# Weight sums of the first up tile by adding DMAs, its norm factor in the second tile, and a final factor kept in PSUM

## The chip, the core and the metric

The kernel runs on one core of one Trainium2 chip. The metric is the device time of one execution in microseconds (us); lower is better. Five engines work side by side, each with its own queue: TensorE (PE, matmuls into PSUM), VectorE (DVE), ScalarE (ACT), GpSimd (POOL) and SyncE (SP, which only issues DMAs). ACT and POOL issue DMAs too.

## The reference

One layer of a decoder trunk, in float32, on 512 tokens of width 2048: a mixer of three head groups, a cross-attention into 256 memory tokens, a gated MLP with a causal convolution of width 3, and a final norm. What the change touches is the MLP and the final norm:

```python
def rms_norm(x, g):
    return x * rsqrt(mean(x * x, axis=-1) + EPS) * g

def conv_ffn(h, w_up, conv_w, conv_b, w_down):      # D_FF = 5504 = 43 tiles of 128
    val, gate = split(h @ w_up, 2, axis=-1)
    gp = pad(gate, two zero tokens in front)
    g = conv_b + sum(conv_w[i] * gp[:, i:i + S] for i in range(3))
    return (silu(g) * val) @ w_down

x = x + hybrid_mixer(rms_norm(x, norm_mix), ...)
x = x + memory_cross_attention(rms_norm(x, norm_cross), mem_n, ...)
x = x + conv_ffn(rms_norm(x, norm_ffn), w_up, conv_w, conv_b, w_down)
return rms_norm(x, norm_final)
```

## The kernel before

Everything is kept transposed: a tile has 128 features on the partitions and the tokens along the free dimension. The residual x lies in 16 tiles of 128x512 (`self.x1`, called str in the profile).

**Precision.** Each operand of a matmul is split in two parts, hi (ScalarE copies it, rounded) and lo (VectorE subtracts: L316/L317 and L341/L342 for weights, tiles whi and wlo with 5 buffers each). A product is three matmuls (hi x hi, lo x hi, hi x lo; L355 to L357). So each 128x512 piece of weights costs one ScalarE and one VectorE operation. Weights come through five buffers `wraw` of 128x1024, loaded on SP's queue.

**The up projection** (`up`, 43 tiles f) computes val and gate of two halves of the tokens by a scheme of seven products in place of eight. The products are numbered 1 to 7. Their left sides are the four units of the tile's weights (b11, b12, b22, b21, units 4f to 4f + 3 of `w_up`, 512 KB each) and sums of them: product 5 takes b11 + b12, product 6 b11 + b12 + b22, product 4 b11 + b12 + b22 + b21, product 7 b12 + b22. In each tile VectorE makes these four sums in place, as 128x1024 additions (L1180, L1185 and helper line L1256). Their right sides are sums of token blocks of x (`token_sums`, tiles called sum), made once while the cross-attention's output projection (`w_co`) runs. The products collect in PSUM tiles acc (products 1, 6, 7), psE or acc (2), psC (5 and 3) and psD (4).

**The first up tile** is begun in `cross`: its products 1, 2, 5 and 6 stand there between the last token sums, in the order `UP_ORDER` = 1, 5, 2, 6, 3, 4, 7 of the sums. `one(0)` in `up` takes the rest over through `self.first`. The norm factor R of the MLP's input isn't put into the weights' right sides; it is multiplied into the gate at L1300 and into the down projection's output. It comes from the squares of x, which ScalarE makes (xsqt, three buffers) and which POOL's adding DMAs collect in two tiles sq (L1140). `rms` adds over the partitions (four matmuls into psT, L450/L451, which `behind()` queues behind the last product on PE), loads ScalarE's table for Ln and Exp, and `root` makes R by Ln, Exp (L463, L464) and three VectorE operations (L465 to L467). In tile 0 `rms` is called between products 3 and 4.

Behind its products each tile has the work on the gate: gate times R (L1300), three convolution steps (L1302 to L1304), Silu, times val, and a store to DRAM (gd).

**The end.** The last three blocks of the down projection are done for each half of the tokens on its own (`finish(hf, dt)`, psD, 16 tiles dt of 128x256): VectorE adds the product to x (L1399), ScalarE squares it, VectorE and POOL collect the squares (fsq). `write(hf)` then makes x times gain times R into tiles o of two dt each and sends them out, 256 KB a DMA, on SP's and ACT's queues by turns; POOL multiplies some dt (L1418), for which ScalarE has put the gain into x (L1407), VectorE the others (L1420). The first half's writing runs between the second half's `finish` calls. For the second half the squares are added by L1437 on PE, then `root`, then `write(1)` ends the kernel.

**Order.** A planner orders each engine's instructions before the run, by readiness in its own model of time and then by place in the program; `issue_after` pins an instruction behind another one on its engine. Engines then run their queues in order.

Of the kernel before, what the change touches and what calls it, by code (L numbers as in the profile page):

```python
# [40 lines left out]
FT = D_FF // P  # L41
# [18 lines left out]
WR = 5  # L60
# [13 lines left out]
H0 = 4  # L74
H1 = 6
ST = 4
FINE = 2
E0 = 14
E1 = 1
W0 = 6  # L80
# [133 lines left out]
class _Trunk:  # L214
# [222 lines left out]

        return rs, spread

    def rms(self, parts, n, pool, after=None):  # L440

        nc = self.nc
        ss = self.pst("T")[:, :n]
        for i, a in enumerate(parts):
            hi = self.wp.tile([P, n], F32R, name="shi", tag="whi", bufs=WS, padded_shape=[P, 512])
            lo = self.wp.tile([P, n], F32R, name="slo", tag="wlo", bufs=WS, padded_shape=[P, 512])
            last = nc.scalar.activation(hi, a, AF.Copy)
            nc.vector.tensor_tensor(lo, a, hi.bitcast(F32), op=ALU.subtract)
            with self.behind():
                nc.tensor.matmul(ss, self.onesr, hi, start=(i == 0), stop=False)  # L450
                nc.tensor.matmul(ss, self.onesr, lo, start=False, stop=(i == len(parts) - 1))  # L451
        self.log_table(after or last)
        return self.root(ss, n, pool, *parts)
# [5 lines left out]
    def root(self, ss, n, pool, r, u):  # L459

        nc = self.nc
        R = pool.tile([P, n], F32, name="R", tag="R", bufs=1)
        nc.scalar.activation(r, ss, AF.Ln, scale=1.0 / D, bias=self.eps)  # L463
        nc.scalar.activation(r, r, AF.Exp, scale=-0.5)  # L464
        nc.vector.scalar_tensor_tensor(u, ss, D * EPS, r, op0=ALU.add, op1=ALU.mult)  # L465
        nc.vector.scalar_tensor_tensor(u, u, -0.5 / D, r, op0=ALU.mult, op1=ALU.mult)
        nc.vector.scalar_tensor_tensor(R, u, 1.5, r, op0=ALU.add, op1=ALU.mult)  # L467
        return R

# [520 lines left out]
    def cross(self):  # L990
# [29 lines left out]
        for i, u in enumerate(first):  # L1020
            more((i >= H0) + (i >= H1))
            u()
            if i == ST:
                R = self.rms(self.sqs, S, self.con)
        more(KT)
        self.es_mp.close()
        es_o, es_w = ExitStack(), ExitStack()
# [60 lines left out]
        def evac_q(h, t0, tn):  # L1088
# [54 lines left out]
        for u in range(8):  # L1143
            w = ws[u]
            pss = [self.acc(), self.acc()]
            for half in range(2):
                for k in range(4):
                    wh, wl = w((half * 4 + k) * P, P)
                    self.mm3(pss[half], wh, wl, oT[k][0], oT[k][1], k == 0, k == 3)
                dt = 2 * u + half  # L1150
                x1 = self.x1[dt]
                nc.vector.tensor_tensor(x1, pss[half], x1, op=ALU.add)
            if u + 2 < 8:
                ws.append(self.weights(d["w_co"][u + 2]))
            elif u == 6:
                b11, b12 = [self.up_raw(i) for i in (0, 1)]
                w1 = self.halves(b11)
            else:
                b21, b22 = [self.up_raw(i) for i in (3, 2)]
                es_o.close()  # L1160
                self.es_fa = ExitStack()
                put(self.pool(self.es_fa, "fa", "left"), own)
            if u % 2:
                part = self.token_sums(u // 2, wx, place)
                if u < 7:
                    for j in UP_ORDER:
                        part(j)
            if u:
                squares(2 * u - 2)
# [4 lines left out]
        part(1)  # L1174
        self.product(1, w1, pa, True, True)
        nc.scalar.activation(s1, pa, AF.Copy)
        w2 = self.halves(b21)
        part(2)
        self.product(2, w2, pe, True, True)
        nc.vector.tensor_tensor(b11, b11, b12, op=ALU.add)  # L1180
# [4 lines left out]
        nc.vector.tensor_tensor(b11, b11, b22, op=ALU.add)  # L1185
# [37 lines left out]
    def up_raw(self, u, pool=None):  # L1223
        if pool:
            t = pool.tile([P, 1024], F32, name="b22", tag="b22", bufs=2)
        else:
            t = self.wp.tile([P, 1024], F32, name="wraw", tag="wraw", bufs=WR)
        self.nc.sync.dma_start(out=t, in_=self.d["w_up"][u])
        return t

    def halves(self, w):
# [10 lines left out]
    def up(self):  # L1242

        nc, d = self.nc, self.d
# [3 lines left out]
        for g in gps:  # L1248
            nc.gpsimd.memset(g[:, 0:2], 0.0)
        lo, hi = slice(0, HT), slice(HT, S)  # L1250

        def cw(i, f):
            return self.conv[:, i * FT + f:i * FT + f + 1]

        def tt(out, a, b, op):
            nc.vector.tensor_tensor(out, a, b, op=op)  # L1256
# [4 lines left out]
        def one(f):  # L1261
            u2, val, gp = tmp("u2"), tmp("val", S, 2), gps[f % 2]
            pd = self.pst("D")[:, :HT]
            if f == 0:
                b11, b12, b21, b22, pb, pc, pe, s1, s5 = self.first
# [18 lines left out]
            tt(b12, b12, b22, ALU.add)  # L1284
# [5 lines left out]
            if f == FT - 1:  # L1290
                self.early = [self.wp.tile([P, 2, S], F32, name="wraw", tag="wraw", bufs=WR) for _ in range(2)]
                for i, t in enumerate(self.early):
                    for k in range(2):
                        nc.sync.dma_start(out=t[:, k, :], in_=self.gd[2 * i + k])
            self.product(7, self.halves(b12), pb, False, True)
            u3 = tmp("u2")
            tt(u3, s1, pb, ALU.subtract)
            tt(val[:, hi], u3, pd, ALU.add)
            tt(gp[:, 2 + HT:], u3, s5, ALU.add)
            nc.vector.scalar_tensor_tensor(gp[:, 2:], gp[:, 2:], -1.0, self.R, op0=ALU.mult, op1=ALU.mult)  # L1300
            c = fb.tile([P, S], F32, name="cv", tag="cv", bufs=2)
            nc.scalar.activation(c, gp[:, 0:S], AF.Identity, scale=cw(0, f), bias=cw(3, f))  # L1302
# [20 lines left out]
    def ffn(self):  # L1323
# [67 lines left out]
        def finish(hf, dt):  # L1391
# [11 lines left out]
                sqs[1].append(sq)  # L1403
            else:
                self.square(dt, x, sqs[hf], lambda n: fp.tile([P, n], F32, name="fsqt", tag="fsqt", bufs=2))
            if dt % 4 == 3 or (hf == 0 and dt % 2):
                nc.scalar.activation(x, x, AF.Copy, scale=self.gain(3, dt))  # L1407
            return added

        def write(hf):  # L1410
            tok = toks[hf]
            R = spreads[hf]
            for dt in range(0, KT, 2):
                o = fp.tile([P, 2, tw], F32, name="o", tag="o", bufs=7)
                for i in range(2):
                    x = self.x1[dt + i][:, tok]
                    if (dt + i) % 4 == 3 or (hf == 0 and i):
                        nc.gpsimd.tensor_tensor(o[:, i, :], x, R, op=ALU.mult)  # L1418
                    else:
                        nc.vector.scalar_tensor_tensor(o[:, i, :], x, self.gain(3, dt + i), R,  # L1420
                                                       op0=ALU.mult, op1=ALU.mult)
                    if hf and dt < FINE:
                        (nc.sync if i else nc.scalar).dma_start(out=self.out[(dt + i) * P:(dt + i + 1) * P, tok],
                                                                in_=o[:, i, :])
                if hf == 0 or dt >= FINE:
                    dst = self.out[dt * P:(dt + 2) * P, tok].rearrange("(i p) t -> p i t", p=P)
                    (nc.sync if dt % 4 else nc.scalar).dma_start(out=dst, in_=o)
                yield

        spreads = {}  # L1430
        w0 = write(0)
# [49 lines left out]
```

## Time and profile before

| | us |
|---|---|
| runs: median (lowest to highest) of 3 | 2361.35 (2359.89 to 2363.28) |
| the profiled execution | 2363.64 |
| its span, first to last instruction | 2361.7 |
| PE busy | 2333.6 |
| DVE busy | 1646.7 |
| ACT busy | 1135.6 |
| POOL busy | 95.4 |

The mean granted TensorE clock is 0.995 of full speed. All times of rows are counted from the span's start. A busy share is a mean over stages; what the change can do is read from the stages that it touches: the first up tile (1009 to 1039 us) and the end (from 2310 us). In a row of a timeline stand the start, the duration, the engine, the line, the operation with output and inputs, the shape, and in brackets how long the engine was idle before and what released it.

### The profile page before, as it was taken

The numbers are of one execution on the slowest core, as the hardware profiler recorded it, in microseconds if no ns is written. First come the engines' busy times: TensorE is split into PE (matmuls) and PEld (weight loads), VectorE is DVE, ScalarE is ACT, GpSimd is POOL, SyncE is SP. The second block draws the span as 40 slices with busy tenths as digits, with TensorE's granted clock in tenths as the row PEclk, the third lists the DMA queues.
The fourth block names the chain that finished last, engine by engine and source line by source line (L and its number), as shares of the span: only waits on it lengthen the run. The fifth ranks groups of instructions, "written<-read, shape, count | busy, mean of one in ns | idle before, by whom it ended". The sixth has DMA issues, their size and how long they took to land.

```text
span 2361.7 us, 38190 instructions
## 1 busy us (share of the span) xinstructions
PE 2333.6 (99%) x14514; PEld 2110.2 (89%) x14514; DVE 1646.7 (70%) x3062; ACT 1135.6 (48%) x2201; POOL 95.4 (4%) x112
## 2 busy tenths in 40 slices
PE   9999999999999999999999999999999999999997
PEld 8798898888878888889999999999999988888887
DVE  7725666667796365898888888888899844343336
ACT  6323345556664254765555555555555532232224
POOL 2000000000002000100000000000000000000003
PEclk9999999999999999999999999999999999999999
DMA  6432122322224343443333333333333443242332
GB/s 208 144 94 88 48 96 90 98 85 94 90 78 155 125 144 117 106 131 121 121 121 121 121 121 121 121 121 120 117 119 118 162 138 125 98 156 95 111 107 72
DMA packets 88452, 272.84 MB, mean 116 GB/s; under 512 B 10012, under 2 KB 14764, under 8 KB 88268
## 3 DMA queue, kind: packets, MB, share of 16 engines
q1 hardware_dynamic: 77200, 250.45, 32.1%
q10 hardware_dynamic: 7772, 12.09, 1.6%
q0 software_dynamic: 3296, 7.87, 1.4%
q8 instruction: 114, 1.87, 0.3%
q14 instruction: 70, 0.57, 0.1%
HBM read 251.18 MB, written 19.45 MB: 115 GB/s over the span
## 4 chain that ended last, share of the span: by engine, by line
PE 94%; DVE 3%; ACT 1%; POOL 1%; DMA 1%; issue 1%; DVEq 0%; SPq 0%; POOLq 0%; ACTq 0%
PE acc L355 18%; PE acc L356 18%; PE acc L357 18%; PE psC L355 3%; PE psC L357 3%; PE psC L356 3%; PE acc L398 3%; PE acc L396 3%; PE acc L397 3%; PE psD L357 2%; PE psD L355 2%; PE psD L356 2%; PE psV L355 2%; PE psU L356 2%; PE psV L356 2%; PE psU L355 2%
## 5 line engine op out<-in xcount | busy, mean ns | idle before, releaser
L342 DVE TENSOR_TENSOR wlo<-wraw,whi 128x512 fp32r<-128x512 f32 (+2 forms) x496 | 333.6, 677 | 413.8 <-ACT whi L341 406.0
L341 ACT ACTIVATE whi<-wraw 128x512 fp32r<-128x512 f32 (+2 forms) x496 | 304.1, 617 | 624.2 <-PE acc L356 366.9
L316 ACT ACTIVATE whi<-wraw 128x512 fp32r<-128x512 f32 x518 | 308.3, 627 | 307.0 <-DVE wraw L1256 161.7
L355 PE MATMUL acc<-xhi,whi 128*128 128x512 f32 (+1 forms) x1088 | 428.9, 395 | 0.0
L357 PE MATMUL acc<-xhi,wlo 128*128 128x512 f32 (+1 forms) x1088 | 423.8, 390 | 0.0
L356 PE MATMUL acc<-xlo,whi 128*128 128x512 f32 (+1 forms) x1088 | 423.2, 389 | 0.0
L317 DVE TENSOR_TENSOR wlo<-wraw,whi 128x512 fp32r<-128x512 f32 x518 | 348.1, 687 | 74.9 <-ACT whi L316 65.8
L357 PE MATMUL acc<-sum,wlo 128*128 128x256 f32 x1368 | 384.9, 281 | 0.1
L356 PE MATMUL acc<-sum,whi 128*128 128x256 f32 x1368 | 384.7, 281 | 0.0
L355 PE MATMUL acc<-sum,whi 128*128 128x256 f32 x1368 | 384.3, 281 | 0.0
L357 PEld LDWEIGHTS acc<-sum,wlo 128*128 128x128 f32 x1368 | 258.0, 189 | 0.6 <-DVE wlo L317 0.6
L356 PEld LDWEIGHTS acc<-sum,whi 128*128 128x128 f32 x1368 | 257.9, 189 | 0.2
L355 PEld LDWEIGHTS acc<-sum,whi 128*128 128x128 f32 x1368 | 257.8, 188 | 0.0
L357 PEld LDWEIGHTS acc<-xhi,wlo 128*128 128x128 f32 x1088 | 205.3, 189 | 42.7 <-issue 0.8
L356 PEld LDWEIGHTS acc<-xlo,whi 128*128 128x128 f32 x1088 | 205.5, 189 | 39.9 <-issue 1.6
L355 PEld LDWEIGHTS acc<-xhi,whi 128*128 128x128 f32 x1088 | 205.4, 189 | 38.8 <-issue 0.8
L357 PE MATMUL psC<-sum,wlo 128*128 128x256 f32 x688 | 193.7, 282 | 0.5 <-DVE wlo L317 0.5
L356 PE MATMUL psC<-sum,whi 128*128 128x256 f32 x688 | 193.0, 280 | 0.4 <-DVE sum L1217 0.4
L355 PE MATMUL psC<-sum,whi 128*128 128x256 f32 x688 | 193.4, 281 | 0.0
L356 PEld LDWEIGHTS psC<-sum,whi 128*128 128x128 f32 x688 | 129.9, 189 | 0.6 <-DVE sum L1217 0.6
L357 PEld LDWEIGHTS psC<-sum,wlo 128*128 128x128 f32 x688 | 129.5, 188 | 0.7 <-DVE wlo L317 0.7
L355 PEld LDWEIGHTS psC<-sum,whi 128*128 128x128 f32 x688 | 129.9, 189 | 0.0
(347 smaller groups left out, 4287.4 us busy)
## 6 DMA issues: line engine op xcount, KB each, us to landing
wraw<-in_w_up SPq DMA_DIRECT2D x130, 512.0 KB, 4.5
wraw<-in_w_dn SPq DMA_DIRECT2D x80, 512.0 KB, 3.7
b<-in_w_up SPq DMA_DIRECT2D x42, 512.0 KB, 3.9
wraw<-in_w_o SPq DMA_DIRECT2D x32, 512.0 KB, 3.6
wraw<-in_w_qka SPq DMA_DIRECT2D x24, 512.0 KB, 3.7
gd<-cv SPq DMA_DIRECT2D x43, 256.0 KB, 2.1
wraw<-in_w_qkb SPq DMA_DIRECT2D x16, 512.0 KB, 3.7
xraw<-in_xT SPq DMA_DIRECT2D x15, 512.0 KB, 3.9
```

The lines of the kernel that those rows point to most:

```text
L316: nc.scalar.activation(hi, r, AF.Copy)
L317: nc.vector.tensor_tensor(lo, r, hi.bitcast(F32), op=ALU.subtract)
L341: nc.scalar.activation(hi, r, AF.Copy)
L342: nc.vector.tensor_tensor(lo, r, hi.bitcast(F32), op=ALU.subtract)
L355: nc.tensor.matmul(out, lh, rh, start=start, stop=False, skip_group_check=more)
L356: nc.tensor.matmul(out, lh, rl, start=False, stop=False, skip_group_check=more)
L357: last = nc.tensor.matmul(out, ll, rh, start=False, stop=stop, skip_group_check=more)
L396: self.nc.tensor.matmul(o, xh[:, tt], wh, start=(k == 0), stop=False)
L397: self.nc.tensor.matmul(o, xh[:, tt], wl, start=False, stop=False)
L398: self.last = self.nc.tensor.matmul(o, xl[:, tt], wh, start=False, stop=(k == KT - 1))
```

## The change

- `first_sums` makes the sums of the first up tile in DRAM: for products 5, 6, 4 and 7 a plain DMA copies the first unit into a DRAM tile (pre5, pre6, pre4, pre7), and seven adding DMAs add the others, all on POOL's queue. It is called in `cross` before the queries' projection (w_cq).
- The first tile then loads seven units on SP's queue, where it loaded four, and VectorE makes no sum of weights there.
- `rms` is cut in three (`sums_of`, `log_table`, `root`). In tile 0 `sums_of` stands behind product 4; `root`, and the gate's work of tile 0 (`gate`), stand in tile 1 between its products 1 and 5.
- At the end R goes to PSUM (`self.acc()`), ScalarE copies it to SBUF for POOL (Rs), the results are written over x, and each dt goes out by a DMA of its own, 128 KB. POOL takes the dt with dt % 3 == 2 in the first half (5 in place of 8) and dt % 5 == 4 in the second (3 in place of 4).

```diff
-    def rms(self, parts, n, pool, after=None):
+    def rms(self, parts, n, R, after=None):
+        ss = self.sums_of(parts, n)
+        self.log_table(after or self.high)
+        self.root(ss, n, R, *parts)
+        return R
...
+        first = self.first_sums()
         for h in range(X_HEADS - 1):
             self.run(self.out_units(d["w_cq"], h, hs, evac_q(h, 0, NT)), W_X)
...
             elif u == 6:
-                b11, b12 = [self.up_raw(i) for i in (0, 1)]
-                w1 = self.halves(b11)
+                w1 = self.halves(self.up_raw(first[1]))
             else:
-                b21, b22 = [self.up_raw(i) for i in (3, 2)]
+                raws = [self.up_raw(first[j]) for j in (2, 5, 6)]
...
-        nc.vector.tensor_tensor(b11, b11, b12, op=ALU.add)
-        w5 = self.halves(b11)
+        w5 = self.halves(raws[1])
...
-        nc.vector.tensor_tensor(b11, b11, b22, op=ALU.add)
-        w6 = self.halves(b11)
+        w6 = self.halves(raws[2])
...
-        self.first = b11, b12, b21, b22, pb, pc, pe, s1, s5
+        self.first = [self.up_raw(first[j]) for j in (3, 4, 7)], pb, pc, pe, s1, s5
+
+    def first_sums(self):
+
+        nc, w = self.nc, self.d["w_up"]
+        terms = {5: (0, 1), 6: (0, 1, 2), 4: (0, 1, 2, 3), 7: (1, 2)}
+        src = {1: w[0], 2: w[3], 3: w[2]}
+        for j in terms:
+            src[j] = self.dr.tile([P, 1024], F32, name="pre%d" % j)
+            nc.gpsimd.dma_start(out=src[j], in_=w[terms[j][0]])
+        for i in (1, 2, 3):
+            for j in terms:
+                if i < len(terms[j]):
+                    nc.gpsimd.dma_start(out=src[j], in_=w[terms[j][i]], accum_op=ALU.add, max_dma_last_dim=1024)
+        return src
...
                 tt(b11, b11, b12, ALU.add)
+                if f == 1:
+                    self.root(self.ss, S, self.R, *self.sqs)
+                    gate(*self.late)
                 self.product(5, self.halves(b11), pc, True, True)
...
             if f == 0:
-                self.R = self.rms(self.sqs, S, self.con)
-            tt(b11, b11, b21, ALU.add)
-            self.product(4, self.halves(b11), pd, True, True)
...
+                w4 = self.halves(t4)
+                self.product(4, w4, pd, True, True)
+                self.ss = self.sums_of(self.sqs, S)
+                w7 = self.halves(t7)
+                self.log_table(self.high)
+                self.product(7, w7, pb, False, True)
...
-            if dt % 4 == 3 or (hf == 0 and dt % 2):
+            if on_pool(hf, dt):
                 nc.scalar.activation(x, x, AF.Copy, scale=self.gain(3, dt))
             return added
+        def on_pool(hf, dt):
+            return dt % 5 == 4 if hf else dt % 3 == 2
+
         def write(hf):
             tok = toks[hf]
...
+            R, Rs = spreads[hf], fp.tile([P, tw], F32, name="R", tag="R", bufs=1)
+            nc.scalar.activation(Rs, R, AF.Copy)
+            for dt in range(KT):
+                x = self.x1[dt][:, tok]
+                if on_pool(hf, dt):
+                    nc.gpsimd.tensor_tensor(x, x, Rs, op=ALU.mult)
+                else:
+                    nc.vector.scalar_tensor_tensor(x, x, self.gain(3, dt), R, op0=ALU.mult, op1=ALU.mult)
+                (nc.sync if dt % 2 else nc.scalar).dma_start(out=self.out[dt * P:(dt + 1) * P, tok], in_=x)
+                if dt % 2:
+                    yield
...
-                spreads[0] = self.rms(sqs[0], tw, fp, self.silu)
+                spreads[0] = self.rms(sqs[0], tw, self.acc()[:, :tw], self.silu)
...
-        spreads[1] = self.root(ss, tw, fp, *sqs[1][:2])
+        spreads[1] = self.acc()[:, :tw]
+        self.root(ss, tw, spreads[1], *sqs[1][:2])
```

More of the change, by code (lines that the diff above doesn't have):

```diff
@@ L76 @@
 ST = 4
-FINE = 2
 E0 = 14
@@ L451, in rms @@
                 nc.tensor.matmul(ss, self.onesr, lo, start=False, stop=(i == len(parts) - 1))
-        self.log_table(after or last)
-        return self.root(ss, n, pool, *parts)
+        return ss
     def log_table(self, after):
@@ L1023, in cross @@
             if i == ST:
-                R = self.rms(self.sqs, S, self.con)
+                R = self.rms(self.sqs, S, self.con.tile([P, S], F32, name="R", tag="R"))
         more(KT)
@@ L1250, in up @@
         lo, hi = slice(0, HT), slice(HT, S)
+        self.R = self.con.tile([P, S], F32, name="R", tag="R")
         def cw(i, f):
@@ L1264, in one @@
             if f == 0:
-                b11, b12, b21, b22, pb, pc, pe, s1, s5 = self.first
+                (b22, t4, t7), pb, pc, pe, s1, s5 = self.first
                 tt(val[:, lo], s1, pe, ALU.add)
@@ L1283, in one @@
             self.product(3, self.halves(b22), pc, False, True)
-            tt(b12, b12, b22, ALU.add)
             tt(gp[:, 2:2 + HT], pc, u2, ALU.add)
             if f == 0:
-                self.R = self.rms(self.sqs, S, self.con)
-            tt(b11, b11, b21, ALU.add)
-            self.product(4, self.halves(b11), pd, True, True)
[L1290 to L1295, printed above, removed]
+                w4 = self.halves(t4)
[5 more added lines that the diff above has]
+            else:
+                tt(b12, b12, b22, ALU.add)
+                tt(b11, b11, b21, ALU.add)
+                self.product(4, self.halves(b11), pd, True, True)
+                if f == FT - 1:
+                    self.early = [self.wp.tile([P, 2, S], F32, name="wraw", tag="wraw", bufs=WR) for _ in range(2)]
+                    for i, t in enumerate(self.early):
+                        for k in range(2):
+                            nc.sync.dma_start(out=t[:, k, :], in_=self.gd[2 * i + k])
+                self.product(7, self.halves(b12), pb, False, True)
             u3 = tmp("u2")
@@ L1299, in one, with gate @@
             tt(gp[:, 2 + HT:], u3, s5, ALU.add)
+            if f:
+                gate(f, gp, val)
+            else:
+                self.late = f, gp, val
+        def gate(f, gp, val):
             nc.vector.scalar_tensor_tensor(gp[:, 2:], gp[:, 2:], -1.0, self.R, op0=ALU.mult, op1=ALU.mult)
@@ L1405, in finish @@
                 self.square(dt, x, sqs[hf], lambda n: fp.tile([P, n], F32, name="fsqt", tag="fsqt", bufs=2))
-            if dt % 4 == 3 or (hf == 0 and dt % 2):
+            if on_pool(hf, dt):
                 nc.scalar.activation(x, x, AF.Copy, scale=self.gain(3, dt))
             return added
+        def on_pool(hf, dt):
+            return dt % 5 == 4 if hf else dt % 3 == 2
         def write(hf):
             tok = toks[hf]
[L1412 to L1428, printed above, removed]
+            R, Rs = spreads[hf], fp.tile([P, tw], F32, name="R", tag="R", bufs=1)
[4 more added lines that the diff above has]
+                    nc.gpsimd.tensor_tensor(x, x, Rs, op=ALU.mult)
+                else:
+                    nc.vector.scalar_tensor_tensor(x, x, self.gain(3, dt), R, op0=ALU.mult, op1=ALU.mult)
+                (nc.sync if dt % 2 else nc.scalar).dma_start(out=self.out[dt * P:(dt + 1) * P, tok], in_=x)
+                if dt % 2:
+                    yield
         spreads = {}
```

11 lines of the change are left out of this document (5 added, 6 removed).

## The prediction

> **What bounds the kernel now.** I read the page first: the span, the busy shares, the chain that ended last.
>
> ```profile
> span 2361.7 us, 38190 instructions
> PE 2333.6 (99%) x14514; PEld 2110.2 (89%) x14514; DVE 1646.7 (70%) x3062; ACT 1135.6 (48%) x2201; POOL 95.4 (4%) x112
> PE 94%; DVE 3%; ACT 1%; POOL 1%; DMA 1%; issue 1%; DVEq 0%; SPq 0%; POOLq 0%; ACTq 0%
> ```
>
> TensorE is busy 99% of the span, and 94% of the chain is its matmuls. An edit on another engine can gain only where TensorE stands still: 28 us in all. The change touches two such places, the first up tile and the end. So I cut windows at the first tile's first matmul and at the first matmuls of the tiles behind it (columns: length, busy of PE, PEld, DVE, ACT, POOL, clock, DMA share, GB/s).
>
> ```profile
> 1009.40:1038.90 29.50, 24.83 (x173) 22.33 (x172) 28.39 (x43) 18.98 (x34) 3.63 (x6) 0.94 0.58 151
> 1038.90:1058.80 19.90, 19.90 (x171) 19.90 (x170) 18.37 (x28) 11.66 (x20) 0.00 (x0) 1.00 0.38 120
> 1058.80:1078.70 19.90, 19.90 (x171) 19.90 (x170) 17.89 (x28) 10.68 (x19) 0.00 (x0) 1.00 0.37 121
> ```
>
> A tile takes 19.90 us with TensorE full; the first takes 29.50, with VectorE busy 28.39 of it. The waits of TensorE there and VectorE's timeline (start, duration, [idle before]) say why:
>
> ```profile
> PE psD L355 <- ACT whi L316: 2.0, 1, 2.0
> PE psT L451 <- DVE slo L448: 1.4, 2, 1.2
> PE psC L357 <- DVE wlo L317: 0.5, 1, 0.5
> PE psC L356 <- DVE sum L1217: 0.4, 1, 0.4
> ```
>
> ```profile
> 1012.70 1.22 DVE L1180 TENSOR_TENSOR wraw<-wraw 128x1024 f32<-128x1024 f32 x1
> 1016.84 1.22 DVE L1185 TENSOR_TENSOR wraw<-wraw 128x1024 f32<-128x1024 f32 x1
> 1025.31 1.22 DVE L1256 TENSOR_TENSOR wraw<-wraw 128x1024 f32<-128x1024 f32 x1
> 1028.65 1.22 DVE L1256 TENSOR_TENSOR wraw<-wraw 128x1024 f32<-128x1024 f32 x1
> 1030.76 0.69 DVE L465 SCALAR_TENSOR_TENSOR sq<-psT,sq 128x512 f32<-128x512 f32 x1 [0.90 <-ACT sq L464]
> 1039.10 0.42 DVE L1256 TENSOR_TENSOR u<-s,acc 128x256 f32<-128x256 f32 x1 [0.32 <-PE acc L357]
> 1049.01 1.29 DVE L317 TENSOR_TENSOR wlo<-b,whi 128x512 fp32r<-128x512 f32 x2
> ```
>
> VectorE feeds TensorE by a hair, and four 1.22 us weight sums stand in its queue.
>
> **The first tile.** The change takes the four sums off VectorE. The next operation starts 1.13 to 1.14 us behind each (pipelined), so 4.6 us go. It moves the three operations L465 to L467 behind the tile, and puts the matmuls of the norm sums (psT) behind product 4.
>
> ```profile
> 1015.87 0.29 PE L355 MATMUL psC<-sum,whi 128*128 128x256 f32 x1
> 2299.89 0.23 PE psU L355
> 1050.28 0.28 PE L355 MATMUL psC<-sum,whi 128*128 128x256 f32 x1
> ```
>
> What can be won: 29.50 - 19.90 = 9.60. Four norm matmuls of 512 columns at 0.23 stay: 0.9. Product 5 starts 6.47 us after 1009.40 where two products take 2/7 of 19.90 = 5.69: that 0.8 belongs to the first splits and stays. So 7.9 us, and tile 2 would start at 1031.0. The lower clock (0.94) goes with the gaps and is in the 7.9.
>
> What is late next is VectorE in tile 2, which gets L465 to L467 (three slots of 0.6) and keeps the first tile's conv work. Its split for product 3 of tile 2 ends at 1049.01 + 1.29 = 1050.3, just when that product starts (1050.28). Without the sums it ends at 1045.7; with the idle 0.90 and 0.32 filled too, at 1044.5. TensorE could be there at 1031.0 + 4 x 2.84 = 1042.4 and needs the first of the two splits, 0.6 us earlier: a stall of 1.5 to 2.7 us. **I take 7.9 - 2.0 = 5.9.** Bounds: 7.9, if the planner puts conv work behind the splits; 3.5, if VectorE also stands waiting for ScalarE's Ln, Exp and Silu in the middle of tile 2's splits, 2 us more.
>
> **What is added there.** Eleven DMAs on POOL's queue: four plain DRAM copies, then seven adding ones on three levels, each level waiting for the one before; and three more 512 KB loads on SP (seven for four). SP's loads of the sums wait for the adds, and the second tile's loads stand behind them: its first takes the slot of product 5's sum, free when product 5 starts (1015.87), 15 us ahead of tile 2. In program order the DMAs stand before w_cq, in a gap of POOL.
>
> ```profile
> 849.09 1.34 POOL L986 TENSOR_TENSOR sq<-sq,sqt 128x512 f32<-128x512 f32 x1 [20.97 <-ACT sqt L984]
> 976.93 1.07 POOL L1140 DMA_DIRECT2D sq<-xsqt  x1 [126.50 <-ACT xsqt L1139]
> sq<-xsqt POOLq DMA_DIRECT2D x14, 256.0 KB, 3.4
> q0 software_dynamic: 2016, 3.67, 30.0%
> q1 hardware_dynamic: 1728, 6.29, 28.4%
> ```
>
> POOL is empty for 126.5 us up to 976.93. No row has a DRAM-to-DRAM add; the nearest is the 256 KB adding DMA above (3.4 us to landing). The two queue rows (packets, MB, share of 16 engines) are of 970 to 1040: 14 adds held the engines for 0.300 x 70 = 21 us, 1.5 each, so 3.0 at 512 KB; a plain load of 512 KB takes 0.284 x 70 / 12 = 1.66. The eleven come to 4 x 1.66 + 7 x 3.0 = 27.6 us of the engines in a gap of 126. I take nothing: matmuls cover it that need 512 KB of weights per 24 x 0.23 = 5.5 us; without that cover, see the first rival. Bounds: 0 and 27.6.
>
> "DMA: Bandwidth & Descriptors" of the Trainium skill, section "Anatomy of one DMA", gives 2.0 us plus bytes over 436 GB/s; by it an estimate for four steps one after the other is 4 x 3.2 = 13 us, and the sum stays.
>
> **The end.** First three groups (count | busy us, mean ns | idle before), then the last instructions in order:
>
> ```profile
> L1399 DVE TENSOR_TENSOR str<-psD,str 128x256 f32<-128x256 f32 x32 | 13.2, 416 | 4.3 <-PE psD L357 4.3
> L1420 DVE SCALAR_TENSOR_TENSOR o<-str,gains,R 128x256 f32<-128x256 f32 x20 | 12.8, 682 | 0.0
> L466 DVE SCALAR_TENSOR_TENSOR fsq<-fsq,fsq 128x256 f32<-128x256 f32 x2 | 0.8, 420 | 0.0
> ```
>
> ```profile
> 2344.83 0.28 PE L357 MATMUL psD<-gkh,xlo 128*128 128x256 f32 x1
> 2346.36 1.13 PE L1437 MATMUL acc<-fsq,ones 128*128 128x256 f32 x4 [1.24 <-POOL fsq L986]
> 2346.51 0.41 DVE L1399 TENSOR_TENSOR str<-psD,str 128x256 f32<-128x256 f32 x1
> 2348.45 0.47 ACT L463 ACTIVATE fsq<-acc,eps 128x256 f32<-128x256 f32 x1 [0.54 <-PE acc L1437]
> 2350.39 0.42 DVE L467 SCALAR_TENSOR_TENSOR R<-fsq,fsq 128x256 f32<-128x256 f32 x1
> 2350.85 6.81 DVE L1420 SCALAR_TENSOR_TENSOR o<-str,gains,R 128x256 f32<-128x256 f32 x12
> 2358.00:2360.00 2.00, 0.00 (x0) 0.00 (x0) 0.00 (x0) 0.00 (x0) 0.00 (x0) 0.50 1.03 345
> ```
>
> L1399 and L1420 have one shape and run side by side while POOL multiplies too; the one that reads PSUM takes 416 ns, the one that reads only SBUF 682. With R in PSUM I take 0.42 for L1420. And POOL gets 5 of the first half's tiles for 8, 3 for 4.
>
> Step one: the last addition waits in VectorE's queue until 2346.51, though its product ends at 2345.11, and TensorE waits for POOL until 2346.36. With both queues shorter the addition starts near 2345.2, the norm matmuls at once, and Ln (2348.45) comes 1.3 us earlier (0 to 1.4). Step two: from R on, VectorE's 13 products take 13 x 0.34 = 4.4 (start to start) for 6.81; but the last window shows the DMA engines full (share 1.03) at 345 GB/s. Half the output, 2.1 MB, needs 6.1 us at that rate; from the first product (2351.4) to 2360 it takes 8.6 now. With the ramp fed faster I take back 1.4 of the 2.5 (0 to 2.5). ScalarE's copy of R for POOL (0.4) delays only POOL's three tiles. The 128 KB DMAs, 16 a half on two queues, issue beside the transfers. **Sum 2.7; bounds 0 and 3.9.**
>
> "Perfetto Trace Analysis" of the Trainium skill, section "Optimizing Scalar/DVE Operations", speaks against R in PSUM: an access overhead of about 125 ns on PSUM, 60 on SBUF. By it 13 products would cost 13 x 65 ns = 0.8 us more, and the gain of the end were 1.9; the trace has 416 ns with PSUM and 420 without (L1399, L466), so I charge nothing.
>
> **Sum.** 5.9 + 2.7 = 8.6. The profiled execution took 2363.6 in all (1.9 beyond its span), 2.3 above the median of the runs, 2361.35; against it 2355.0, against the median 2352.7, which I give. Own range: 3.5 + 0 to 7.9 + 3.9, so 2349.5 to 2357.9.
>
> **The rivals.**
>
> 1. *The eleven DMAs run at the start.* The planner issues what waits for nothing as soon as an engine is free.
>
> ```profile
> 3.87 0.45 ACTq L841 DMA_DIRECT2D conv<-in_conv  x1
> 4.40 1.15 POOL L980 TENSOR_TENSOR ls<-xraw 128x512 f32<-128x512 f32 x1 [3.37 <-DMA xraw<-in_xT]
> 5.00:10.00 5.00, 4.10 (x20) 3.63 (x21) 3.36 (x5) 2.94 (x7) 1.59 (x2) 1.00 0.93 336
> 10.00:15.00 5.00, 4.62 (x26) 4.18 (x25) 4.51 (x7) 4.80 (x10) 2.17 (x2) 1.00 0.91 319
> 20.00:25.00 5.00, 5.00 (x29) 5.00 (x28) 5.00 (x7) 4.08 (x8) 1.75 (x2) 1.00 0.62 192
> ```
>
> conv's load stands in the code behind the whole first projection (its line follows that loop) and ran at 3.87. The four copies wait for nothing, and POOL stands idle 3.37 us before 4.40. There the engines are at 0.93 and 0.91, so the copies' 6.6 us push every load back by as much; the adds' 21 us meet a share of 0.62 and cost between nothing and 14 us, taken 7; POOL's squares queue behind adds that wait for copies. 13.6 us in all: 2366.3, slower (6.6 to 20 us: 2359 to 2373). It decides from 8.6 us of delay on. Against: conv was drawn ahead by some 45 us, the copies would have to be by 870. "DMA: Bandwidth & Descriptors" of the Trainium skill, section "Issuing engines are not separate DMA queues", has all queues' DMAs interleave on the same 16 engines; by that rule the copies do share with the loads. Chance 0.30.
>
> 2. *VectorE takes it back in tile 2.* Norm, conv and splits stand in a bad order, or DMA rate holds the end: only the lower bound of 3.5 stays, 2357.9. For it: VectorE is busy 18.37 of 19.90 in tile 2 already. Chance 0.10.
>
> 3. *POOL's adds end late.* If seven adds take over 126.5 / 7 = 18 us each, POOL is held past 976.93; behind it stand the sq adds, then ScalarE for its three xsqt buffers, then w_co's splits and TensorE. At 21 us each 2352.7 + 20.5 = 2373. Against: 3.4 us for half the size. Chance 0.05.
>
> 4. *It does not do what it says.* The splits wait for ScalarE (the 2.0 row names its whi), so the first tile stays and only the end moves: 2358.7. Against: ScalarE is busy 18.98 of 29.50. Chance 0.05.
>
> **How the numbers follow.** The forecast has 0.50. About 0.2% (4.7 us) is what a measurement here can tell from no change: faster is below 2356.6, slower above 2366.1. Faster: 0.50 and a third of rival 2 (0.03), 0.02 of rival 1, 0.55. Slower: half of rival 1 (0.15) and rival 3, 0.20. The same: 0.25. The range runs from the forecast's lower end to 2368, which leaves out the upper part of rival 1 (0.10) and rival 3.
>
> **What will show it.** Right: 1009 to 1031 holds the first tile in 21 to 23 us, no 128x1024 sum in it, a wait of 1 to 3 us at psC in tile 2; L1420 at 0.42 while POOL works; Ln 2 us behind the last product's end (3.3 now); the copies issued behind 850. Wrong: copies near 1 us and waits for xraw before 45 (rival 1); waits for wlo above 4 us in tile 2 (rival 2); xsqt waits for sq beyond 980 (rival 3); the four waits of the first tile unchanged (rival 4).

## The result, and the profile after

The changed kernel takes 2386.06 us (median of 4 runs, 2382.69 to 2390.84), the one before 2362.18 in the same comparison: ratio 1.0104, 95% interval 1.0085 to 1.0123. It is 24 us slower where 8.6 us faster was forecast, and outside the range that ended at 2368.0. The sign is that of the first rival. The size is beyond it: the rival had at most 20 us of delay over the forecast of 2352.7, and the kernel lies 33 us above it.

First the page of the changed kernel, and its windows over the first up tile, the second and the third, cut at their first matmuls (columns as before).

```profile
span 2389.0 us, 38213 instructions
PE 2344.7 (98%) x14514; PEld 2120.5 (89%) x14514; DVE 1634.0 (68%) x3062; ACT 1133.9 (47%) x2199; POOL 98.8 (4%) x119
PE 93%; DVE 2%; issue 2%; DMA 1%; ACT 1%; POOL 1%; ACTq 0%; DVEq 0%; SPq 0%
```

```profile
1041.94:1064.88 22.94, 21.36 (x174) 20.78 (x173) 20.60 (x35) 17.72 (x32) 3.65 (x6) 1.00 0.94 260
1064.88:1087.61 22.73, 20.97 (x171) 20.15 (x170) 20.75 (x32) 12.62 (x22) 0.00 (x0) 1.00 0.31 108
1087.61:1107.51 19.90, 19.90 (x171) 19.90 (x170) 17.90 (x28) 10.68 (x19) 0.00 (x0) 1.00 0.37 121
```

The first tile does what the change says: 22.94 us in place of 29.50, at full clock. The second loses 2.83 (22.73 for 19.90). So the two tiles together win 3.73 of 49.40 (29.50 + 19.90). But its first matmul starts at 1041.94 where it started at 1009.40: the kernel is **32.5 us late before the changed tile begins**. On the page's chain one word has grown, "issue", from 1% to 2% of the span: time in which an engine waited for nothing that the profile shows.

The chain of work in order of time says where (start, duration, what; 20 to 75 us of the changed kernel):

```profile
23.87 1.33 POOL ls L988
25.20 1.05 POOL pre L1206
26.25 9.49 issue
35.74 1.05 POOL pre L1206
36.79 1.28 POOL ls L988
38.07 4.27 issue
42.34 1.02 POOL pre L1206
43.36 5.75 issue
...
64.08 6.64 DMA pre<-in_w_up
70.72 0.40 issue
71.12 1.02 POOL pre L1206
72.15 1.08 POOL rsx L425
```

The chain runs along POOL's queue: an adding DMA (pre), a gap, the next one, an addition of the first norm's squares (ls), a gap. All eleven DMAs were issued at the start, the copies from 1.3 us on, the last add at 71.1. rsx, the first norm factor, comes at the end of that queue, at 71.8 us; before it came at 40.76. What it did to the others stands in the waits of ScalarE up to 75 us and of TensorE up to 110 us (waiting tile, line, what for: us in all, times, longest) and in windows of TensorE's worst stretch, three short ones and the whole:

```profile
ACT ls L986 <- POOL ls L988: 20.4, 3, 10.1
ACT vv L614 <- POOL rsx L425: 10.8, 1, 10.8
ACT xhi L307 <- DMA xraw<-in_xT: 6.3, 4, 3.6
```

```profile
PE acc L395 <- ACT whi L340: 14.5, 3, 7.4
```

```profile
35.00:40.00 5.00, 0.72 (x4) 0.38 (x3) 0.62 (x1) 1.90 (x4) 2.33 (x2) 1.00 0.46 73
45.00:50.00 5.00, 1.93 (x11) 1.59 (x9) 0.00 (x0) 0.00 (x0) 0.89 (x2) 1.00 0.62 97
50.00:55.00 5.00, 0.69 (x1) 0.29 (x1) 2.27 (x4) 3.24 (x6) 1.42 (x2) 0.56 0.87 154
20.00:70.00 50.00, 33.38 (x150) 31.30 (x149) 17.82 (x28) 17.77 (x33) 15.37 (x13) 0.81 0.87 222
```

Read them together. ScalarE squares x into buffers that POOL empties; POOL's additions (L988) stand in its queue behind the adds, so ScalarE waits 20.4 us for them. The splits wait with it, and so does TensorE (14.5 us for whi), which works 0.72 of 5 us between 35 and 40. In that window the DMA engines are busy 0.46 at 73 GB/s: there it is not transfer rate that is short. The wait for loads (xraw, 6.3 us; 5.2 before) is the smaller part. But over the 50 us as a whole the DMA engines are busy 0.87, near the 0.93 and 0.91 of 5 to 15 us before the change. So the profile alone doesn't decide between a held queue and full engines; the experiments below do. TensorE also runs slower between its waits: the granted clock is 0.81 over the 50 us, and over the kernel the same 14514 matmuls keep it busy for 2344.7 us, where they take 2328.5 with the DMAs out of the start (the run "late" below).

The end, in the order of the prediction's rows (last product, Ln, R, VectorE's products):

```profile
2373.65 0.28 PE L356 MATMUL psD<-gkh,xlo 128*128 128x256 f32 x1
2376.84 0.47 ACT L466 ACTIVATE fsq<-acc,eps 128x256 f32<-128x256 f32 x1 [0.85 <-PE acc L1464]
2378.71 0.43 DVE L470 SCALAR_TENSOR_TENSOR acc<-fsq,fsq 128x256 f32<-128x256 f32 x1
2379.59 5.18 DVE L1452 SCALAR_TENSOR_TENSOR str<-str,gains,acc 128x256 f32<-128x256 f32 x13 [0.45 <-ACT R L1446]
```

From the last product's start to the span's end it takes 15.35 us (2389.0 - 2373.65) for 16.87 before: 1.5 won, 0.4 of it ahead of Ln and 1.1 behind. The 13 products take 5.18 us, where before the change 12 took 6.81; from 2384 to 2386 the DMA engines are full again (share 1.03, 338 GB/s).

### The profile page after: what moved, and what is told of

It reads as the page before. It is cut to its first block, busy times and chain, and to the rows that moved or that the text cites. A ratio compares the mean times of both kernels' runs of the same rounds, so it can differ in the third digit from the quotient of the medians.

```text
span 2389.0 us, 38213 instructions
## 1 busy us (share of the span) xinstructions
PE 2344.7 (98%) x14514; PEld 2120.5 (89%) x14514; DVE 1634.0 (68%) x3062; ACT 1133.9 (47%) x2199; POOL 98.8 (4%) x119
## 4 chain that ended last, share of the span: by engine, by line
PE 93%; DVE 2%; issue 2%; DMA 1%; ACT 1%; POOL 1%; ACTq 0%; DVEq 0%; SPq 0%
PE acc L354 18%; PE acc L355 18%; PE acc L356 18%; PE psC L356 3%; PE psC L354 3%; PE psC L355 3%; PE acc L395 2%; PE acc L396 2%; PE acc L397 2%; PE psD L354 2%; PE psD L356 2%; PE psD L355 2%; PE psU L356 2%; PE psU L354 2%; PE psV L355 2%
## 5 line engine op out<-in xcount | busy, mean ns | idle before, releaser
L395 PE MATMUL acc<-whi,xhi 128*128 128x384 f32 (+2 forms) x320 | 118.7, 371 | 16.4 <-ACT whi L340 14.5
```

Of the source, the lines that this page charges most:

```text
L395: self.nc.tensor.matmul(o, xh[:, tt], wh, start=(k == 0), stop=False)
```

## The experiments

**Theory** (queue): POOL issues in order, the planner put the eleven DMAs ahead, and POOL stands in adds that can't go out, with the first norm's additions behind them. **Rival** (bandwidth): the eleven DMAs push the loads of x and of the first weights back by their bytes. Both have the DMAs at the start; they differ in what happens if the bytes stay and the waits go.

### Where the DMAs run, and what of them costs

The run "late" pins all eleven behind POOL's last square of the mixer; "copies_early" pins the adds alone.

```diff
...
-        first = self.first_sums()
+        with tc.issue_after(self.pool_last.ins):
+            first = self.first_sums()
```

> All eleven DMAs are queued behind POOL's last square of the mixer (849 us in the trace of before), all else as changed. The start then has nothing new in it. Queue theory and bandwidth theory agree here: the 32.5 us by which the changed kernel was late at 1009 us go, and what the changed kernel wins behind that point stays (its lead shrinks from 32.5 to 27.3 us, so 5.2): 2362.2 - 5.2 = 2357, 2354 to 2360. If a part of the 32.5 us comes from another place than the start, the time stays above 2362.

> Only the seven adding DMAs are queued behind POOL's last square; the four plain copies stay at 1 to 22 us. Queue theory (POOL stands in adds that wait, and its squares of x behind them): nothing waits, only the copies' 4 x 1.66 = 6.6 us of the DMA engines are left, 0 to 4 us over the run with all eleven late, 2357 to 2361. Bandwidth theory (the eleven push the loads of x and w back by their bytes): 2.1 of 5.8 MB are left, 12 of 32.5 us, about 2369.

"wide" leaves all at the start and changes the pieces of an add; "plain11" takes the adding away, so that the first tile gets single units in place of their sums:

```diff
# wide
-  nc.gpsimd.dma_start(out=src[j], in_=w[terms[j][i]], accum_op=ALU.add, max_dma_last_dim=1024)
+  nc.gpsimd.dma_start(out=src[j], in_=w[terms[j][i]], accum_op=ALU.add, max_dma_last_dim=4096)
# plain11
-  nc.gpsimd.dma_start(out=src[j], in_=w[terms[j][i]], accum_op=ALU.add, max_dma_last_dim=1024)
+  spare = self.dr.tile([P, 1024], F32, name="spare%d%d" % (j, i))
+  nc.gpsimd.dma_start(out=spare, in_=w[terms[j][i]])
```

> All eleven at the start as changed, the same bytes and waits, but an add goes out in 128 pieces of 4 KB where it went in 512 of 1 KB. In the changed kernel each add was issued 0.3 us after the one before it had landed, without a wait that the profile shows. If the number of pieces in flight is what holds it, adds now go out as soon as their copies have landed: under the queue theory the start costs 5 to 15 us in place of 32.5, 2362 to 2372. If the waits for the levels or the bytes hold it, the time stays at 2386.

> All eleven at the start, the seven adds made into plain copies of the same 512 KB into spare DRAM tiles (the first up tile then gets single units in place of their sums): the same bytes read, no DMA that waits for another. Queue theory: 11 x 1.66 = 18 us of the DMA engines, half of it beside free share, 4 to 12 us over the run with all late, 2361 to 2369. Bandwidth theory: 2386 still, or a few us less for the sums' second reading of the tile.

| run | us, median | against before (95%) | over late | DMA engines' time in the eleven, first 110 us |
|---|---|---|---|---|
| late | 2354.92 | 0.9969 (0.9956 to 0.9981) | | 0 |
| copies_early | 2358.61 | 0.9985 (0.9976 to 0.9994) | 3.7 | 5.8 |
| plain11 | 2365.10 | 1.0011 (1.0002 to 1.0021) | 10.2 | 15.3 |
| wide | 2368.94 | 1.0028 (1.0017 to 1.0038) | 14.0 | 24.8 |
| the change itself | 2386.06 | 1.0104 (1.0085 to 1.0123) | 31.1 | 30.7 |

The last row was measured in another comparison than the others (before: 2362.18 there, 2362.17 here). The last column is worked out: the share of the queue that POOL's DMAs use (q0; in this stretch they are the eleven), times 110 us. Two of these rows, of the changed kernel and of wide (packets, MB, share):

```profile
q0 software_dynamic: 3824, 5.77, 27.9%
```

```profile
q0 software_dynamic: 1136, 5.77, 22.5%
```

All four came out as the queue theory has it, and the column "over late" reads like a bill. The four copies cost 3.7 us; seven more plain transfers 6.5 on top (10.2 - 3.7); the adding and the waits between the levels 3.8 (14.0 - 10.2); and 17.1, more than half, goes with the pieces of 1 KB alone (31.1 - 14.0). The step from 10.2 to 14.0 is no larger than the spread of the runs of one kernel and is read with care. The bandwidth theory had 2386 for "wide" and "plain11" and 2369 for "copies_early", and fell.

The bytes of the changed kernel and of wide are the same, and 2688 packets fewer are 7 x 384, which is 512 to 128 for each of seven adds. But smaller pieces also keep the DMA engines longer, 30.7 us for 24.8, and that is a rival for the 17.1. It is too small: in the first three runs of the bill a microsecond of the engines costs about 0.6 us of the kernel, so 5.9 us more would cost 3 to 4, and 5.9 if each counted in full. The other 11 to 14 are an estimate of what the held queue costs. The first norm's factor rsx says the same: it comes at 54.63 us in wide, 17.2 us earlier than in the changed kernel (71.79).

For what is left in wide the rival does hold. There ScalarE waits for loads, not for POOL's additions, and the DMA engines' share lies between 1.03 and 1.06 from 25 to 55 us:

```profile
ACT xhi L307 <- DMA xraw<-in_xT: 16.4, 7, 5.5
```

POOL's waits in front of the seven adds, in the changed kernel, in late and in wide ("issue": no wait that the profile shows):

```profile
POOL pre L1206 <- issue: 29.9, 5, 9.5
POOL pre L1206 <- DMA pre<-in_w_up: 4.7, 1, 4.7
```

```profile
POOL pre L1209 <- issue: 42.8, 5, 10.7
POOL pre L1209 <- DMA pre<-in_w_up: 10.4, 2, 7.7
```

```profile
POOL pre L1206 <- DMA pre<-in_w_up: 4.8, 2, 3.2
```

In late the hold-up is still there, 42.8 us of it, from 852 to 909, and costs nothing: POOL has nothing to do until 973. With 4 KB pieces it is gone even at the start. So an add in 512 pieces isn't issued until the one before it has landed: in the changed kernel the adds go out 6 to 11 us apart, one takes 6.4 us to land in the median (10.3 at most), and the next goes out about 0.3 us behind the landing. Adds in 128 pieces don't wait so: in the run "best" below, four of them go out within 5 us, and none lands in less than 4.4. What runs full isn't seen in a trace. "DMA: Bandwidth & Descriptors" of the Trainium skill, section "SWDGE vs HWDGE vs iDMA", has GpSimd write the descriptors of its DMAs into rings in SBUF that the DMA engines empty; by that, a full ring would fit the rows, though the page doesn't say that POOL waits for it. The kernel sets a size for these descriptors (dynamic_dma_scratch_size=2048); another one wasn't tried, so the resource that runs out stays open.

### One constant behind the adds

Is it the first norm that makes the start so dear, or any work behind the adds? "after_pow" pins the eleven behind POOL's pow of that norm (L425, 41 us), where the DMA engines have share to spare.

```diff
+        op = nc.gpsimd.tensor_tensor(rs, rs, self.mhalf[:, :tl], op=ALU.pow)
+        if name == "x":
+            self.pow_x = op
...
-        with tc.issue_after(self.pool_last.ins):
+        with tc.issue_after(self.pow_x.ins):
```

> The eleven DMAs are queued behind POOL's pow of the first norm (41 us), adds in pieces of 1 KB. Nothing of the first norm stands behind them any more, and the DMA engines have 0.2 to 0.4 of share there, but POOL's constants for the next stage (used from about 96 us on) stand behind adds that are held for 57 us or more. Queue theory: the delay is what these constants are late, 41 + 5 + 60 = 106 us for a use at 96 to 100, so 5 to 12 us over all late: 2360 to 2367. Bandwidth theory: free share takes the bytes up, 2355 to 2357.

2373.08 us, 1.0041 (1.0026 to 1.0057), and 19.7 over late2 (below), in the same comparison: more than expected, and by another instruction than the one named there. POOL's timeline, TensorE's longest wait between 30 and 160 us, and a window:

```profile
58.35 1.04 POOL L1211 DMA_DIRECT2D pre<-in_w_up  x1 [10.57 <-issue]
65.18 1.02 POOL L1211 DMA_DIRECT2D pre<-in_w_up  x1 [5.79 <-issue]
71.30 1.03 POOL L1211 DMA_DIRECT2D pre<-in_w_up  x1 [5.10 <-issue]
71.93 0.51 POOL L657 MEMSET fone<- 8x512 f32 x1
```

```profile
PE psT L665 <- DVE cn L659: 14.8, 1, 14.8
```

```profile
60.00:80.00 20.00, 6.16 (x15) 3.86 (x16) 4.80 (x8) 1.15 (x2) 3.18 (x4) 0.54 0.60 100
```

A constant of 8x512, 0.5 us of work, is made at 71.93; in late2 POOL writes it at 54.13. VectorE's scan (cn) needs it, TensorE needs the scan, and waits 14.8 us. In that window the DMA engines are busy 0.60, and the granted clock is 0.54; in the two windows of 20 us behind it it is 0.84 and 0.85, where late2 has 1.00. That may account for the rest of the 19.7. So it is the queue again, and not the bytes.

### The parts that were meant to win

"late" is the change as its text reads, so its parts are taken out of it one by one.

"end_back" has the end of before, "sbuf_r" keeps the new end but leaves R in SBUF:

```diff
# sbuf_r
-            R, Rs = spreads[hf], fp.tile([P, tw], F32, name="R", tag="R", bufs=1)
-            nc.scalar.activation(Rs, R, AF.Copy)
+            R = Rs = spreads[hf]
...
-        spreads[1] = self.acc()[:, :tw]
+        spreads[1] = fp.tile([P, tw], F32, name="R", tag="R", bufs=1)
```

> As the run with all eleven late (2354.9), with the end of before: R in SBUF, results in tiles of their own, POOL with 8 and 4 tiles. The forecast's term for the end was 2.7: 2357.6. By the two traces (the stretch from tile 2 to the span's end is 1.5 us shorter in the changed kernel) 2356.4. If the end gave nothing, 2354.9.

> As the run with all eleven late (2354.9), but R stays in SBUF in both halves (no copy for POOL); results in place and POOL's 5 and 3 tiles stay. Theory: VectorE's products go from 0.40 apart to 0.50 or more while POOL multiplies, so they last 6 us in place of 5.2 and the end comes 0.5 to 1.5 us later: 2355.4 to 2356.4. Rival: the output's DMAs at 340 GB/s hold the end anyway, and ScalarE's copy of R is saved: 2354.5 to 2355.

end_back took 2357.36 (0.9977, 0.9968 to 0.9986), sbuf_r 2356.46 (0.9978, 0.9969 to 0.9987): by the medians the end is worth 2.4 us and R in PSUM 1.5 of it, by the ratios 1.9 and 2.1. Against the second run of late (late2 below, 2353.37) it would be 4.0 and 3.1. That is at the edge of what the runs tell apart: some 2 us or more, and R in PSUM most of it. The traces are sharper: from the last product's start to the span's end it takes 15.32 us in late, 16.75 in sbuf_r, 17.15 in end_back, so 1.8 for the end and 1.4 of it for R in PSUM. Two groups each of late and of sbuf_r, 2310 to 2360 us:

```profile
L1455 DVE SCALAR_TENSOR_TENSOR str<-str,gains,acc 128x256 f32<-128x256 f32 x24 | 10.1, 471 | 0.5 <-ACT R L1449 0.5
L1453 POOL TENSOR_TENSOR str<-str,R 128x256 f32<-128x256 f32 x8 | 5.7, 741 | 5.9 <-ACT R L1449 5.8
```

```profile
L1454 DVE SCALAR_TENSOR_TENSOR str<-str,gains,R 128x256 f32<-128x256 f32 x24 | 13.8, 625 | 0.0
L1452 POOL TENSOR_TENSOR str<-str,R 128x256 f32<-128x256 f32 x8 | 6.9, 891 | 5.9 <-DVE R L470 5.9
```

One operand moved from SBUF to PSUM, and both engines are faster, VectorE by 154 ns a product and POOL by 150. "SBUF — State Buffer" of the Trainium skill, section "SBUF: two separate sides", says that a VectorE operation with two SBUF inputs and a GpSimd operation that reads SBUF exclude each other on a shared pair of ports; these rows agree. That two SBUF inputs alone make VectorE slow is ruled out by a product of sbuf_r itself, made while POOL stands idle (2336.6 to 2338.5): it takes no longer than one with R in PSUM.

```profile
2337.88 0.47 DVE L1454 SCALAR_TENSOR_TENSOR str<-str,gains,R 128x256 f32<-128x256 f32 x1
```

"norm_back" makes the norm factor between products 3 and 4 again and puts the gate's work of tile 0 behind tile 0:

```diff
+                self.rms(self.sqs, S, self.R)
                 w4 = self.halves(t4)
                 self.product(4, w4, pd, True, True)
-                self.ss = self.sums_of(self.sqs, S)
...
-                if f == 1:
-                    self.root(self.ss, S, self.R, *self.sqs)
-                    gate(*self.late)
```

> As the run with all eleven late (2354.9), but the norm factor is made between products 3 and 4 of the first tile as before, and the gate's work of tile 0 stands behind tile 0. If the move is needed for the gain, the waits for the norm in the first tile (1.4 at psT and 2.0 at psD before) come back and tile 2 loses its stall of 2.8: 2354 to 2358. If the four sums on VectorE were the whole hold-up, the split for product 4 is early enough anyway and the stall in tile 2 goes: 2352 to 2354.

2359.07 us (0.9986, 0.9977 to 0.9995), above both expectations. Its windows over the first two tiles, then those of late:

```profile
1005.51:1031.24 25.73, 23.36 (x173) 22.25 (x172) 22.09 (x38) 17.51 (x31) 3.50 (x6) 0.93 0.81 232
1031.24:1053.39 22.15, 20.70 (x171) 20.08 (x170) 19.62 (x30) 12.77 (x22) 0.00 (x0) 1.00 0.34 108
```

```profile
1006.00:1027.89 21.89, 21.55 (x173) 20.91 (x172) 21.04 (x36) 18.05 (x33) 3.66 (x6) 1.00 0.93 252
1027.89:1050.65 22.76, 20.99 (x171) 20.17 (x170) 20.77 (x32) 12.64 (x22) 0.00 (x0) 1.00 0.38 128
```

Without the move the first tile is 25.73 long and the second keeps its stall, 22.15: the sums alone win 1.5 of 49.40. With the move the two are 44.65, 4.75 less than before. The sums and the move together win 4.75, so the move is needed for most of it; the move without the sums wasn't tried.

"gate_p3" leaves the sums and the move, and places root and the gate's work of tile 0 later in tile 1, behind product 3:

```diff
-                if f == 1:
-                    self.root(self.ss, S, self.R, *self.sqs)
-                    gate(*self.late)
                 self.product(5, self.halves(b11), pc, True, True)
...
             tt(gp[:, 2:2 + HT], pc, u2, ALU.add)
+            if f == 1:
+                self.root(self.ss, S, self.R, *self.sqs)
+                gate(*self.late)
```

> As the run with all eleven late (2354.9), but root and the gate's work of tile 0 are placed behind product 3 of tile 1, not before its product 5. There TensorE lost 2.8 us against four full products (11.4 us): waits for splits at products 5 and 6. Theory: VectorE's and ScalarE's work on R and the gate stands in front of these splits, so they come earlier and 1.5 to 2.8 us go: 2352 to 2353.5. Rival: the same work is then late for product 4 or for tile 3, and the stall only moves: 2354.5 to 2355.5.

2353.31 us (0.9961, 0.9948 to 0.9973). Its windows over the same tiles:

```profile
1007.37:1028.77 21.40, 21.39 (x174) 20.87 (x172) 20.92 (x36) 17.93 (x33) 3.52 (x6) 1.00 0.96 259
1028.77:1048.68 19.91, 19.91 (x171) 19.91 (x170) 19.81 (x31) 12.12 (x22) 0.00 (x0) 1.00 0.43 133
```

TensorE is full in both, and the second tile has its 19.91 back. The stretch wins 8.09 of 49.40, 3.3 more than late. So the stall of tile 2 came from the place of the gate's work in front of the splits. Nothing comes late in its stead: from the first tile's start to the span's end it is 1342.6 us in gate_p3, for 1346.0 in late. The medians show less of it, 1.6 us against late and nothing against its second run (late2, 2353.37), so whole runs don't show this gain clear of their noise. The profiled execution of gate_p3 reached its first tile 1.4 us later than that of late (1007.37 and 1006.00), and such differences at the start (last section) are as large as the gain.

### The two together

"best" is gate_p3 with adds in pieces of 4 KB; "late2" is late once more, in the same comparison.

> All eleven DMAs behind POOL's last square once more, so that the two runs beside it have it on the same chip: 2355, 2353.5 to 2356.5.

> All eleven late, root and the gate's work of tile 0 behind product 3 of tile 1, and the adds in 128 pieces of 4 KB. Where adds of 1 KB pieces were held in the gap (42.8 us of idle POOL before five of the seven without a wait that the profile shows), the theory of the pieces in flight has none of that: the seven adds are out within 35 us in place of 57. The time is that of the 1 KB pieces, 2352 to 2353.5, since nothing waits for POOL there. If the hold-up stays, it is not the number of pieces.

late2 took 2353.37 (0.9964, 0.9952 to 0.9977), a little under its expected range. best took 2352.48 (0.9958, 0.9946 to 0.9971): faster than both kernels of this case, 9.5 us ahead of before, and 0.9 ahead of late2, which such medians can't tell apart for sure. From the first tile's start to the span's end the traces have 1343.1 us in best and 1345.1 in late2, so the later place of the gate's work is worth 2.0 here, and 3.4 between gate_p3 and late. POOL's adds in best, all seven out within 30 us where they took 58 in late:

```profile
L1209 POOL DMA_DIRECT2D pre<-in_w_up x7 | 5.8, 822 | 26.6 <-DMA pre<-in_w_up 26.6
```

No "issue" is left in that row; all of the idle time is waiting for the level before.

## Why the prediction was wrong, point by point

- **What bounds the kernel, and the first tile: right in the mechanism, the term too large.** It forecast 21 to 23 us for the first tile, 7.9 won there, 2.0 lost in tile 2, 5.9 in all. The changed kernel has 22.94, 6.56, 2.83 and 3.73; late has 21.89, 7.61, 2.86 and 4.75. The stall was taken too small and at another place: not at psC for product 3, but for splits of products 5 and 6, because R and the gate's work stand ahead of them in program order. That is near what the prediction gave as the condition of its lower bound (3.5): in late ScalarE loads a table (1.28 us) and makes Silu just ahead of the splits for which TensorE then waits 1.0. One premise was too narrow: time is won not only where TensorE stands still. Its busy time in the first tile falls as well, from 24.83 at a granted clock of 0.94 to 21.36 at 1.00.
- **The end: right in kind, 2.7 forecast, 1.5 in the trace and some 2 by the runs.** VectorE's products fell to 471 ns for the 0.42 us taken (682 before). Step one was the weak one, 0.4 won for 1.3: Ln stands 2.9 us behind the last product's end for the 2 forecast, since VectorE still had three operations in front of the last addition. In step two the prediction set 13 products against a row of 12, and took 4.4 us for them; they take 5.18, and 1.1 was won for 1.4.
- **What is added there: this step failed.** The term for the eleven DMAs was put at nothing. "I take nothing" rested on POOL's gap up to 976.93, that is, on the program's order. The planner issued the eleven from 1.3 us on, the first norm's additions stood behind adds that were held, and the first up tile began 32.5 us late; the runs price the step at 31.1. With the DMAs in the gap (late) the time is 2354.92, and 2353.37 in its second run, near the forecast of 2352.7. That nearness is in part luck. In late's trace the two terms of the forecast come to 4.75 + 1.5 = 6.3 us for 8.6, and executions differ ahead of all that the change adds: POOL's last square of the mixer comes at 845.67 us in late's trace and at 849.09 in before's.
- **The first rival: the right mechanism, at less than half its price.** Its three signs were there: copies near 1 us, waits for xraw before 45, POOL's squares behind adds. Its 13.6 us is near what "wide" cost, 14.0, by chance: it took 6.6 for the copies and 7 for the adds, and they cost 3.7 and 10.3. The engines' time was priced well, 27.6 us for 24.8 in wide and 30.7 in the changed kernel. What it left out is the time for which adds in 512 pieces hold POOL itself, most of the other 17.1. The nearest row was the sq adds of before, 886 ns each and issued close behind one another; they go in fewer pieces (2016 packets for 14 of them, 144 each), so they never showed it.
- **Its chance of 0.30 was too low.** The argument against it, that conv was drawn ahead by 45 us and the copies would have to be by 870, says nothing: an instruction that waits for nothing has no distance at which it stops being ready.
- **Rivals 2 to 4** didn't decide: tile 2 took 2.8 us back, not all; the adds did hold POOL, in late for 58 us, but well short of 973; of the four waits of the first tile only the smallest, 0.3 to 0.4 for a token sum, was left in late.

## What to carry to other kernels

Work without inputs doesn't stay where the program puts it: under a planner that goes by readiness, pin it behind an instruction of its own queue, and look in the trace where it ran. Price a DMA on a computing engine's queue twice, once in bytes and once in the time for which it can hold that queue; here a 0.5 us constant behind four adds cost 15 us with the DMA engines at 0.60. And when an engine is freed in one stage, look at what the program then puts first in the next: moving the gate's work behind product 3 won 2 to 3.4 us in the traces, for 4.75 of the sums and the norm's move.

## What the runs showed of the hardware

An add of 512 KB in 512 pieces of 1 KB kept the next one from being issued for 4 to 11 us, without a wait in the profile; in 128 pieces of 4 KB it did not. And executions of equal work differ by some 3 us in the first 100 us alone: POOL's constant ke comes at 95.34 us in end_back and at 98.58 in sbuf_r. Up to 840 us late and sbuf_r do the same work; their windows from 80 to 100 us:

```profile
80.00:100.00 20.00, 20.00 (x88) 16.41 (x88) 16.24 (x28) 6.78 (x12) 0.99 (x2) 1.00 0.72 268
```

```profile
80.00:100.00 20.00, 20.00 (x77) 15.87 (x77) 13.39 (x22) 6.40 (x11) 0.99 (x2) 0.88 0.65 244
```

TensorE is busy throughout in both, but the granted clock is 0.88 in sbuf_r, which gets 77 matmuls done for 88, and ke there comes at 98.58 for 96.14. "TensorE: Matmul & The Clock Gate" of the Trainium skill, section "Part 1: The HAM clock gate", says that the window by which the clock is set runs free, so that the slow stretch at a kernel's start differs from run to run. The rows show a clock that differs between executions of equal work; that the window's phase is the reason, no run here shows. For a change worth some us, compare stretches cut at the same instructions, as above, before whole spans.
